# A front and a layer border that transpose the residual itself, in a two-layer f32 trunk on one core

## The chip, the core and the metric

The kernel runs on one core of a Trainium2 chip. Five engines work side by side: TensorE (PE in the profile; its weight loads are PEld), VectorE (DVE), ScalarE (ACT), GpSimd (POOL) and SyncE (SP), which only issues transfers. Matmuls write PSUM, of which the kernel uses eight banks of 128 x 512 f32; everything else stands in SBUF. The metric is device microseconds of the whole program; lower is better.

## The reference, cut to what matters

```
h = rms_norm(x, norm_pre[layer])                 # x: (1, 512, 2048) f32
even layer: z = h @ w_in (2048 x 7168): qa, fa, ia, ga, ub, vb, gb
            8 recurrence heads from qa, fa, ia (values), gate ga
            8 spatial-gating groups from ub, vb (layer-normed), gate gb
            y = concat @ w_out (2048 x 2048)
odd layer:  z = h @ w_in: cq (512), ckv (512), kpe (64), gate (2048)
            q = rms_norm(cq) @ w_qb,  kv = rms_norm(ckv) @ w_kvb
            16 heads of causal attention, times silu(gate);  y = o @ w_out
x = x + rms_norm(y, norm_post[layer])
```

`rms_norm(x, w)` multiplies each row by one factor r = (mean(x^2) + eps)^-0.5 and each column by w. Both factors can be put elsewhere: w into the rows of the next weight matrix, r onto the rows of the product.

## The kernel before

All large products are made with three matmuls on operands split in two parts of type fp32r: high x high, high x low, low x high. The activations' transposes stand in `R`, 32 slots of 128 x 512, high and low part for each of 16 blocks k of the model dimension. Weights come in tiles of 128 x 1024 f32 (`raw`, three buffers, 512 KB each), are cast to `whi` on ACT (L168) and their remainder `wlo` is made on DVE (L169), four buffers each; `piece(n)` asks for tile n + 3 before tile n is used.

Products of two kinds are made. `proj_tok` (L209 to L211) holds four row blocks of 128 tokens as weights of the array and streams 256 or 512 columns of the weight matrix: the values ia, vb, cq, ckv and both output projections. `proj_feat` (L214 to L216) holds the weight matrix and streams 512 tokens: fa, qa, ga, ub, gb and the gate. A 512 wide `proj_tok` takes four `mm` banks, all there are with that name; `sc` and `tp` have two each.

The front: for each of four row blocks `pre_norm` squares four chunks of x (L290), adds (L292), forms the factor on POOL (L275, L276), multiplies by factor and norm weight on DVE (L296), transposes 16 times on PE (L301) and splits into `R` (L283, L284). The norm weight is loaded into four partitions and spread by stream shuffles. Head values are projected in three chunks: pair 0 with 256 columns, pairs 1 and 2 together with 512, pair 3 with 256. The first chunk runs with its first four weight tiles in one group, row block by row block.

The border: `out_proj` makes the even layer's output in four chunks of 512 columns. Each evacuation squares (L674) and multiplies by the post-norm weight (L675). After the last chunk of a row block, `last_evac` adds the squares (L680), forms the factor on POOL, adds the residual (L684), stores x1 and calls `pre_norm` for the odd layer, whose scaling and transposes are put off by six to seven ticks (`DEFER`); a tick passes with each weight tile or part of a group. The chunk cq follows.

Nobody writes the order out: the framework's scheduler places instructions on each engine by priority and by its own estimate of when they can run; the `at(delay, ...)` tasks only set where they are handed to it. All DMAs go through SP in one queue.

## Time and profile before

| | us |
|---|---|
| median of 3 runs (lowest, highest) | 1597.62 (1597.39, 1598.52) |
| profiled execution: its own time | 1596.93 |
| its span, first to last instruction | 1595.2 |
| PE busy | 1568.3 |
| DVE busy | 750.8 |
| ACT busy | 532.0 |
| POOL busy | 95.7 |

A row of the groups reads: line, engine, operation, output<-inputs, shape, count | busy us, mean ns of one | idle time of the engine just before them and what ended it. A row of the timeline begins with the start and the duration in us. Matmul ends are modelled, so the step from start to start tells more than a duration. Numbers Lnnn are lines of the kernel before; the order of the changed kernel has its own line numbers.

### The profile page before, as it was taken

To read this page: it belongs to the slowest core of one execution; us is meant where nothing else is said; L and a number is where in the kernel's file an instruction comes from. 1 tells how busy PE (TensorE), PEld (TensorE's weight loads), DVE (VectorE), ACT (ScalarE), POOL (GpSimd) and SP (SyncE) were. 2 spreads that over 40 slices of the span, in tenths; PEclk is the share of its full clock that TensorE was granted. 3 is DMA by queue.
4 is the path that set the end of the run, shared out by engine and by line. 5 is a ranking of instruction groups with operands and counts; after the bars stand their busy time and mean duration, and the time that the engine had idled before them with its cause. 6 is when DMAs were issued, how large, how long until landed. Compare 5 with 4: busy or idle time off the path is not lost. (4 is left out here: it accounts for less than half of the span.)

```text
span 1595.2 us, 19593 instructions
## 1 busy us (share of the span) xinstructions
PE 1568.3 (98%) x7841; PEld 1327.2 (83%) x7841; DVE 750.8 (47%) x1333; ACT 532.0 (33%) x904; POOL 95.7 (6%) x145
## 2 busy tenths in 40 slices
PE   6999999999999999999999999999999999999997
PEld 6888888898888888888887788888889988988886
DVE  7653455535434224353225743232266767762234
ACT  6422322222222222232224533222265555542221
POOL 1000000000014004000001000000000000000000
PEclk9999999999999999999999999999999999999999
DMA  7332222223234333243335523333221221332324
GB/s 221 118 92 80 92 93 80 80 80 99 91 102 119 99 98 101 94 151 100 102 103 172 150 78 102 93 93 98 87 75 55 70 60 52 102 106 94 105 93 158
DMA packets 118150, 160.95 MB, mean 101 GB/s; under 512 B 7830, under 2 KB 74408, under 8 KB 118056
## 3 DMA queue, kind: packets, MB, share of 16 engines
q1 hardware_dynamic: 118060, 159.71, 32.4%
q8 instruction: 61, 1.00, 0.3%
q14 instruction: 29, 0.24, 0.0%
HBM read 151.30 MB, written 8.39 MB: 100 GB/s over the span
## 5 line engine op out<-in xcount | busy, mean ns | idle before, releaser
L169 DVE TENSOR_TENSOR wlo<-raw,whi 128x1024 fp32r<-128x1024 f32 x240 | 296.8, 1238 | 641.3 <-ACT whi L168 624.8
L168 ACT CAST whi<-raw 128x1024 fp32r<-128x1024 f32 x240 | 252.3, 1052 | 779.1 <-PE mm L211 346.3
L209 PE MATMUL mm<-whi,R 128*128 128x512 f32 (+1 forms) x960 | 364.0, 379 | 0.5 <-ACT R L283 0.5
L210 PE MATMUL mm<-wlo,R 128*128 128x512 f32 (+1 forms) x960 | 362.1, 377 | 1.2 <-DVE wlo L169 1.2
L211 PE MATMUL mm<-whi,R 128*128 128x512 f32 (+1 forms) x960 | 362.1, 377 | 0.0
L214 PE MATMUL mm<-R,whi 128*128 128x512 f32 x832 | 326.1, 392 | 0.0
L216 PE MATMUL mm<-R,wlo 128*128 128x512 f32 x832 | 324.0, 389 | 0.0
L215 PE MATMUL mm<-R,whi 128*128 128x512 f32 x832 | 323.9, 389 | 0.0
L210 PEld LDWEIGHTS mm<-wlo,R 128*128 128x128 f32 x960 | 181.6, 189 | 33.3 <-DVE wlo L169 2.0
L209 PEld LDWEIGHTS mm<-whi,R 128*128 128x128 f32 x960 | 181.6, 189 | 33.0 <-ACT R L283 1.2
L211 PEld LDWEIGHTS mm<-whi,R 128*128 128x128 f32 x960 | 181.5, 189 | 32.5
L216 PEld LDWEIGHTS mm<-R,wlo 128*128 128x128 f32 x832 | 156.1, 188 | 32.6
L214 PEld LDWEIGHTS mm<-R,whi 128*128 128x128 f32 x832 | 156.2, 188 | 32.2
L215 PEld LDWEIGHTS mm<-R,whi 128*128 128x128 f32 x832 | 156.2, 188 | 32.0
L214 PE MATMUL mm<-Wc,whi 128*128 128x512 f32 x160 | 62.9, 393 | 0.0
L216 PE MATMUL mm<-Wc,wlo 128*128 128x512 f32 x160 | 62.6, 391 | 0.0
L215 PE MATMUL mm<-Wc,whi 128*128 128x512 f32 x160 | 62.4, 390 | 0.0
L284 DVE TENSOR_TENSOR R<-mm,R 128x512 fp32r<-128x512 f32 x48 | 32.9, 686 | 27.9 <-ACT R L283 27.9
L284 DVE TENSOR_TENSOR R<-tp,R 128x512 fp32r<-128x512 f32 x64 | 42.3, 684 | 4.2 <-ACT R L283 3.5
L283 ACT CAST R<-tp 128x512 fp32r<-128x512 f32 x64 | 35.9, 587 | 20.4 <-PE tp L301 18.2
L896 ACT ACTIVATE G<-sc,nm 128x512 f32<-128x512 f32 (+2 forms) x48 | 26.1, 545 | 41.2 <-DVE nm L895 41.2
L283 ACT CAST R<-mm 128x512 fp32r<-128x512 f32 x48 | 28.2, 587 | 32.2 <-PE mm L211 18.3
(243 smaller groups left out, 1645.9 us busy)
## 6 DMA issues: line engine op xcount, KB each, us to landing
raw<-in_ev_w_in_dram SPq DMA_DIRECT2D x112, 512.0 KB, 3.6
raw<-in_od_w_in_dram SPq DMA_DIRECT2D x49, 512.0 KB, 3.8
raw<-in_ev_w_out_dram SPq DMA_DIRECT2D x32, 512.0 KB, 3.6
raw<-in_od_w_out_dram SPq DMA_DIRECT2D x32, 512.0 KB, 3.7
raw<-in_od_w_kvb_dram SPq DMA_DIRECT2D x16, 512.0 KB, 3.6
raw<-in_od_w_qb_dram SPq DMA_DIRECT2D x16, 384.0 KB, 3.2
Wa<-in_x_dram SPq DMA_DIRECT2D x16, 256.0 KB, 6.3
G<-in_x_dram SPq DMA_DIRECT2D x16, 256.0 KB, 4.2
```

Source lines behind the costliest of these rows:

```text
L168: nc.scalar.copy(hi[:, 0:n], raw[:, 0:n])
L169: nc.vector.tensor_tensor(lo[:, 0:n], raw[:, 0:n], hi[:, 0:n].bitcast(F32), ALU.subtract)
L209: nc.tensor.matmul(o, hh[:, sl], wh, start=first, stop=False, skip_group_check=True)
L210: nc.tensor.matmul(o, hh[:, sl], wl, start=False, stop=False, skip_group_check=True)
L211: nc.tensor.matmul(o, hl[:, sl], wh, start=False, stop=last, skip_group_check=True)
L214: nc.tensor.matmul(ps, hi, hh, start=first, stop=False)
L215: nc.tensor.matmul(ps, hi, hl, start=False, stop=False)
L216: nc.tensor.matmul(ps, lo, hh, start=False, stop=last)
L283: nc.scalar.copy(dst_hi, src)
L284: nc.vector.tensor_tensor(dst_lo, src, dst_hi.bitcast(F32), ALU.subtract)
L896: nc.scalar.activation(pv[j], sp[j], AF.Exp, bias=nm[:, j:j + 1], scale=C_SCALE, accum_out=su[:, j:j + 1])
```

## The change

*Raw-block front.* x is transposed as it is. `flip_x` transposes two 128 x 128 blocks, ACT scales them by the norm weight while it casts them into `R` (a column per partition, `ncol`), DVE makes the low parts. `first_chunk` runs the first value chunk, now 512 wide, in eight pieces of four turns; a turn has six matmuls, one flip ahead and, in four of the pieces, a square. Six and eight idle transposes of the identity stand at its beginning. The row factor rn is known after the seventh piece; it is applied in each evacuation of the even layer, as an ACT scale, or as a DVE multiplication by `rb`, the factor spread over all partitions by four small matmuls. The layer norm of vb takes eps times the mean square instead. Values are projected 512 wide for pairs 0 and 1, and 2 and 3.

*Border.* The last output chunk's second half and the first half of cq run in eight turns written by hand, one row block each; the transposes (`flip_x1`) read the sum x1 itself. The odd layer's norm weight is multiplied into its weight tiles (`normed`), the row factor goes into the evacuations and, for cq and ckv, into the epsilon of their norms.

*Order.* Inside the two stretches `in_order` ties every PE, ACT and DVE instruction to the one traced before it; several loads are held in program order on SP. Setup of masks, rope and columns is handed over later.

```diff
+    def in_order():
...
+        for ins in traced[start:]:
+            if ins.engine in (mybir.EngineType.PE, mybir.EngineType.Activation, mybir.EngineType.DVE):
+                if ins.engine in prev:
+                    tc.add_manual_dep(ins, prev[ins.engine],
+                                      mybir.DependencyInfo(mybir.DependencyClass.NoSync,
+                                                           mybir.DependencyReason.DATA), reason="in_order")
+                prev[ins.engine] = ins.name
...
-    for c in range(4):
-        (nc.vector if c % 2 else nc.gpsimd).memset(B[:, 4 + c, :], 0.0)
-    nc.sync.dma_start(out=B[0:P:32, 4:8, :],
-                      in_=norm_pre[0].partition_broadcast(4).rearrange("q (c n) -> q c n", c=4))
-    for c in range(4):
-        nc.sync.dma_start(out=W[:, c, :], in_=x_t[0][:, c * 512:(c + 1) * 512])
+    nrow = B[0:16, 0, 0:P]
+    nc.sync.dma_start(out=nrow, in_=norm_pre[0].rearrange("(k p) -> k p", p=P))
+    def load_x(i, c):
+        tc.keep_in_program_order(nc.sync.dma_start(out=W[:, 4 * i + c, :],
+                                                   in_=x_t[i][:, c * 512:(c + 1) * 512]))
+    load_x(0, 0)
...
+        if i in norm_k:
+            for kk in range(nk):
+                e = slice(kk * nco, (kk + 1) * nco)
+                w = cols[:, 18 + norm_k[i] + kk:19 + norm_k[i] + kk]
+                nc.scalar.activation(hi[:, e], raw[:, e], AF.Copy, scale=w)
+                nc.vector.scalar_tensor_tensor(lo[:, e], raw[:, e], w, hi[:, e].bitcast(F32),
+                                               ALU.mult, ALU.subtract)
...
+        if cuts is None or cuts == "halves":
...
+    def square(i, c):
+        nc.scalar.activation(G[:, 7, :], W[:, 4 * i + c, :], AF.Square, scale=D ** -0.5,
+                             accum_out=pss[:, i, c:c + 1])
+    def factor():
+        nc.vector.tensor_reduce(rms[:, 2], pss, AX.X, ALU.add)
+        nc.gpsimd.tensor_scalar(rms[:, 2], rms[:, 2], EPS, None, ALU.add)
+        nc.gpsimd.tensor_tensor(rn, rms[:, 2], mhalf[:, 0:4], ALU.pow)
+        nc.gpsimd.tensor_scalar(eps_rn, rms[:, 2], EPS, None, ALU.mult)
+    def spread_rn():
+        tp = tp_bank()
+        for i in range(NT):
+            nc.tensor.matmul(tp[:, i * P:(i + 1) * P], rn[:, i:i + 1].broadcast_to([P, P]), ident,
+                             start=True, stop=True)
+        nc.scalar.copy(rb, tp)
+    def flip_x(n):
+        q, i = n // NT, n % NT
+        if q > 7:
+            return
+        tp = tp_bank()
+        sl = slice(i * P, (i + 1) * P)
+        for j in range(2):
+            o = (2 * q + j) % 4 * P
+            nc.tensor.transpose(tp[:, j * P:(j + 1) * P], W[:, 4 * i + q // 2, o:o + P], ident)
+        parts = [(2 * q + j, ncol[:, 2 * q + j:2 * q + j + 1], tp[:, j * P:(j + 1) * P]) for j in range(2)]
+        for k, w, src in parts:
+            nc.scalar.activation(R[:, 2 * k, sl], src, AF.Copy, scale=w)
+        for k, w, src in parts:
+            nc.vector.scalar_tensor_tensor(R[:, 2 * k + 1, sl], src, w, R[:, 2 * k, sl].bitcast(F32),
+                                           ALU.mult, ALU.subtract)
+    def first_chunk(first, evac):
+        outs = [mm_bank() for _ in range(NT)]
+        ntp = sc_bank()
+        nc.tensor.transpose(ntp[:, 0:KD], nrow, ident[0:KD, 0:KD])
+        nc.vector.tensor_copy(ncol, ntp[:, 0:KD])
+        def idle_turns(n):
+            for _ in range(n):
+                nc.tensor.transpose(ntp[:, P:2 * P], ident, ident)
+        idle_turns(6)
+        flip_x(0)
+        idle_turns(8)
+        issue_to(first)
+        flips = iter(range(1, 8 * NT + 4))
+        for q in range(8):
+            if q + 3 < 8:
+                fetch(first + q + 3)
+            if q < 2:
+                for t in range(NT):
+                    load_x(t, 2 + q)
+            for i in range(NT):
+                if q > 0 or i > 1:
+                    flip_x(next(flips))
+                mms(q, i, 0)
+                if q == 0 and i < 2:
+                    flip_x(next(flips))
+                mms(q, i, 1)
+                if q == 0 and i < 2:
+                    flip_x(next(flips))
+                if i == (0 if q else 1) and q < 7:
+                    issue_to(first + q + 1)
+                if q in (1, 3, 4, 6):
+                    square(i, {1: 0, 3: 1, 4: 2, 6: 3}[q])
+                if q == 7:
+                    evac(i, outs[i])
+            if q == 6:
+                factor()
+            tick()
...
-        if p == 1:
-            pl["ia", p] = plan_chunk(ew, IA + 256, 512, KD, 2)
-        elif p != 2:
-            pl["ia", p] = plan_chunk(ew, IA + 256 * p, 256, KD, 4)
+        if p % 2 == 0:
+            pl["ia", p] = plan_chunk(ew, IA + 256 * p, 512, KD, 2, "halves" if p == 0 else None)
...
-    wpre = [B[:, 4 + c, :] for c in range(4)]
-    for c in range(4):
-        nc.vector.stream_shuffle(wpre[c], wpre[c], [0] * 32)
+    fetch(0)
+    for i in range(1, NT):
+        load_x(i, 0)
+    fetch(1)
     for i in range(NT):
-        if i > 0:
-            for c in range(4):
-                nc.sync.dma_start(out=W[:, 4 * i + c, :], in_=x_t[i][:, c * 512:(c + 1) * 512])
-            if i == 1:
-                issue_to(3)
-        else:
-            for q in range(2):
-                fetch(q)
-        pre_norm(i, [W[:, 4 * i + c, :] for c in range(4)], wpre,
...
+        load_x(i, 1)
+        if i == 1:
+            fetch(2)
...
+                nc.scalar.activation(G[:, vp:vp + 2, i * P:(i + 1) * P], psv[:, a:a + 2], AF.Copy,
+                                     scale=rn[:, i:i + 1])
         def fa_evac(m, ps):
+            nc.vector.tensor_tensor(ps, ps, rb, ALU.mult)
             nc.scalar.activation(W[:, m, :], ps, AF.Sigmoid)
             nc.scalar.activation(W[:, 2 + m, :], ps, AF.Sigmoid, scale=-1.0)
         def qa_evac(m, ps):
-            nc.scalar.copy(W[:, 4 + m, :], ps)
+            nc.vector.tensor_tensor(W[:, 4 + m, :], ps, rb, ALU.mult)
...
         if p == 0:
-            at(1, setup_cols)
-            at(12, setup_rope)
-        if p != 2:
-            proj_tok(pl["ia", p], 512 if p == 1 else 256, r_act, KD, ia_evac, by="first" if p == 0 else "piece")
+            at(2, setup_masks)
+            at(7, load_pk)
+            at(9, spread_rn)
+            at(11, setup_cols)
+            at(16, setup_rope)
+            with in_order():
+                first_chunk(pl["ia", p], ia_evac)
+        elif p == 2:
+            proj_tok(pl["ia", p], 512, r_act, KD, ia_evac)
...
-                nc.scalar.copy(U[:, m], ps)
+                nc.vector.tensor_tensor(U[:, m], ps, rb, ALU.mult)
             def gb_evac(m, ps, p=p, Z=Z, V=V):
+                nc.vector.tensor_tensor(ps, ps, rb, ALU.mult)
...
+        def last_sum(i, ps):
             evac(i, ps, 1536, 3)
...
+            rs[i] = rstd_of(s1, D, 1, "yrs")
+        def last_add(i):
...
+                nc.vector.scalar_tensor_tensor(ch[c], ch[c], rs[i], resid[i][c], ALU.mult, ALU.add)
+            finish(i, ch)
             if i + 2 < NT:
                 load_resid(i + 2)
...
+    def flip_x1(i, c):
+        tp = tp_bank() if c % 2 else sc_bank()
+        for j in range(4):
+            nc.tensor.transpose(tp[:, j * P:(j + 1) * P], W[:, 4 * i + c, j * P:(j + 1) * P], ident)
+        sl = slice(i * P, (i + 1) * P)
+        split_into(R[:, 8 * c:8 * c + 8:2, sl], R[:, 8 * c + 1:8 * c + 8:2, sl],
+                   tp.rearrange("p (j t) -> p j t", j=4))
+    def square_x1(i, c):
+        nc.scalar.activation(G[:, 8, :], W[:, 4 * i + c, :], AF.Square, scale=D ** -0.5,
+                             accum_out=pss[:, i, c:c + 1])
...
+    def border(eo, last_sum, last_add):
+        cq = pl["cq"]
+        turns = {(1, 2): [(flip_x1, 0, 0)], (1, 3): [(flip_x1, 0, 1)],
+                 (2, 2): [(flip_x1, 1, 0)], (2, 3): [(flip_x1, 1, 1)],
+                 (4, 1): [(flip_x1, 0, 2)], (4, 2): [(flip_x1, 0, 3)],
+                 (5, 0): [(flip_x1, 2, 0)], (5, 1): [(flip_x1, 2, 1), (last_add, 3)],
+                 (5, 2): [(flip_x1, 1, 2)], (5, 3): [(flip_x1, 1, 3)],
+                 (6, 0): [(flip_x1, 3, 0)], (6, 1): [(flip_x1, 3, 1)],
+                 (6, 2): [(flip_x1, 2, 2)], (6, 3): [(flip_x1, 2, 3)],
+                 (7, 0): [(flip_x1, 3, 2), (issue_to, cq + 4)], (7, 1): [(flip_x1, 3, 3), (issue_to, cq + 5)],
+                 (7, 2): [(issue_to, cq + 6)],
+                 (1, 0): [(last_add, 0)], (2, 0): [(last_add, 1)], (4, 0): [(last_add, 2)]}
+        for j in range(4):
+            turns[3, j] = [(issue_to, cq + j), (fetch, cq + 3 + j)]
...
+        issue_to(eo + 7)
+        for n in range(3):
+            fetch(cq + n)
+        with in_order():
+            for turn in range(8):
+                for j in range(4):
+                    if turn < 4:
+                        mms(outs, eo, 4 + j, turn)
+                    else:
+                        mms(cq_outs, cq, j, turn - 4)
+                    for fn, *args in turns.get((turn, j), ()):
+                        fn(*args)
+                    if j == 3 and turn < NT:
+                        last_sum(turn, outs[turn])
+                    if turn >= NT:
+                        square_x1(turn - NT, j)
+                    tick()
+            factor_x1()
...
+        if first:
+            for q in range(4, 8):
+                wh, wl = piece(pl[name] + q)
...
+                tick()
+        else:
+            proj_tok(pl[name], 512, r_act, KD, evac)
+        r = sm.tile([P, 4], F32, name="lrs")
+        nc.gpsimd.tensor_tensor(r, ss, eps_rn1, ALU.add)
+        nc.gpsimd.tensor_tensor(r, r, mhalf[:, 0:4], ALU.pow)
...
+    spread_rn1()
...
+            nc.vector.tensor_tensor(ps, ps, rb, ALU.mult)```

PE at the start, before (tp: transposed x; mm: the chunk's bank; whi, wlo: parts of the weight tile):

```order
L301 MATMUL tp_123<-ident_90,B_77 128x128 x4
L301 MATMUL tp_131<-ident_90,B_77 128x128 x4
L209 MATMUL mm_332<-whi_158,R_76 128x256
L210 MATMUL mm_332<-wlo_159,R_76 128x256
L301 MATMUL tp_139<-ident_90,B_77 128x128 x4
L211 MATMUL mm_332<-whi_158,R_76 128x256
```

and in the change (sc: a bank for the norm column and the idle transposes; Wa: x as loaded):

```order
L407 MATMUL sc_120<-ident_83,B_77 128x16
L412 MATMUL sc_120<-ident_83 128x128 x6
L390 MATMUL tp_129<-ident_83,Wa_80 128x128 x2
L412 MATMUL sc_120<-ident_83 128x128 x8
L251 MATMUL mm_116<-whi_144,R_76 128x512
L252 MATMUL mm_116<-wlo_145,R_76 128x512
L253 MATMUL mm_116<-whi_144,R_76 128x512
L390 MATMUL tp_159<-ident_83,Wa_80 128x128 x2
```

The transposes read loaded x (Wa) and no longer the scaled copy (B), and come two at a time between threes of matmuls.

ACT at the start, with what each instruction waits for, before:

```order
L290 ACT_TABLE_LOAD
L290 ACTIVATE G_78,pss_112<-Wa_80 128x512 [waits DMAHW0_49]
L290 ACTIVATE G_78,pss_112<-Wa_80 128x512 [waits DMAHW1_49,Activation_49]
L290 ACTIVATE G_78,pss_112<-Wa_80 128x512 [waits DMAHW3_49,Activation_49]
L290 ACTIVATE G_78,pss_112<-Wa_80 128x512 [waits DMAHW4_49,Activation_49]
L168 CAST whi_158<-raw_108 128x1024 [waits DMAHW0_49]
```

and in the change (DVE_49: DVE's counter, here the copy into ncol):

```order
L393 ACT_TABLE_LOAD [waits DVE_49]
L393 ACTIVATE R_76<-tp_129,ncol_90 128x128 [waits PE_49]
L393 ACTIVATE R_76<-tp_129,ncol_90 128x128
L210 CAST whi_144<-raw_97 128x512 [waits DMAHW2_49]
L210 CAST whi_144<-raw_97 128x512
L393 ACTIVATE R_76<-tp_159,ncol_90 128x128 [waits PE_49]
```

The table load had no wait and now stands behind one; the weight cast follows the first flip.

DVE at the border, from the last output chunk's first row block on, before (yrs, prs: row factors; B in L296: the scaled copy):

```order
L675 TENSOR_TENSOR Wa_80<-mm_5706,B_77 128x512
L680 TENSOR_REDUCE ys1_5880<-yss_4905 128x1
L684 SCALAR_TENSOR_TENSOR Wa_80<-Wa_80,yrs_5882,G_78 128x512 x4
L292 TENSOR_REDUCE ps1_5902<-pss_5897 128x1
L296 SCALAR_TENSOR_TENSOR B_77<-Wa_80,prs_5904,B_77 128x512
L675 TENSOR_TENSOR Wa_80<-mm_5707,B_77 128x512
```

and in the change (sc, tp: the transposed sum):

```order
L806 TENSOR_TENSOR Wa_80<-mm_5649,B_77 128x512
L813 TENSOR_REDUCE ys1_5811<-yss_4848 128x1
L819 SCALAR_TENSOR_TENSOR Wa_80<-Wa_80,yrs_5813,G_78 128x512 x4
L326 TENSOR_TENSOR R_76<-sc_5846,R_76 128x4x128
L326 TENSOR_TENSOR R_76<-tp_5859,R_76 128x4x128
L806 TENSOR_TENSOR Wa_80<-mm_5650,B_77 128x512
```

Between the residual sum and the split of its transposes no norm sum and no scaling stands any more.

More of the change, by code (lines that the diff above doesn't have):

```diff
@@ L1 @@
-from contextlib import ExitStack
+from contextlib import ExitStack, contextmanager
 import numpy as np
@@ L117, in setup_cols @@
         tp = tp_bank()
-        nc.tensor.transpose(tp[:, 0:18], pk, ident[0:18, 0:18])
-        nc.scalar.copy(cols, tp[:, 0:18])
+        nc.tensor.transpose(tp[:, 0:34], pk, ident[0:34, 0:34])
+        nc.scalar.copy(cols, tp[:, 0:34])
         e = sm.tile([P, 4, 8], F32, name="lbt", bufs=1)
@@ L166, in wload @@
         lo = ring.tile([P, 1024], F32R, name="wlo", tag="wlo")
-        if cuts is None:
-            nc.scalar.copy(hi[:, 0:n], raw[:, 0:n])
-            nc.vector.tensor_tensor(lo[:, 0:n], raw[:, 0:n], hi[:, 0:n].bitcast(F32), ALU.subtract)
+        if i in norm_k:
[5 more added lines that the diff above has]
+                                               ALU.mult, ALU.subtract)
+            return (hi[:, 0:n].rearrange("p (k c) -> p k c", k=nk),
+                    lo[:, 0:n].rearrange("p (k c) -> p k c", k=nk))
+        if cuts is None or cuts == "halves":
+            step = n if cuts is None else n // 2
+            for a in range(0, n, step):
+                e = slice(a, a + step)
+                nc.scalar.copy(hi[:, e], raw[:, e])
+                nc.vector.tensor_tensor(lo[:, e], raw[:, e], hi[:, e].bitcast(F32), ALU.subtract)
         else:
@@ L702, in out_proj @@
             proj_tok(pl[name, c], 512, r_act, KD, lambda i, ps, c=c: evac(i, ps, c * 512, c))
-        proj_tok(pl[name, 3], 512, r_act, KD, last_evac, by="last")
+        if border:
+            border(pl[name, 3], last_sum, last_add)
+        else:
+            proj_tok(pl[name, 3], 512, r_act, KD, last_evac, by="last")
+    rn1, eps_rn1 = rms[:, 0], rms[:, 1]
     def finish0(i, ch):
-        if i == 0:
-            for c in range(4):
-                row_bc(B[:, 4 + c, :], norm_pre[1, c * 512:(c + 1) * 512])
@@ new lines, in square_x1, with factor_x1, spread_rn1 @@
+    def square_x1(i, c):
+        nc.scalar.activation(G[:, 8, :], W[:, 4 * i + c, :], AF.Square, scale=D ** -0.5,
+                             accum_out=pss[:, i, c:c + 1])
+    def factor_x1():
+        nc.vector.tensor_reduce(rms[:, 2], pss, AX.X, ALU.add)
+        nc.gpsimd.tensor_scalar(rms[:, 2], rms[:, 2], EPS, None, ALU.add)
+        nc.gpsimd.tensor_scalar(eps_rn1, rms[:, 2], EPS, None, ALU.mult)
+        nc.gpsimd.tensor_tensor(rn1, rms[:, 2], mhalf[:, 0:4], ALU.pow)
+    def spread_rn1():
+        tp = tp_bank()
+        for i in range(NT):
+            nc.tensor.matmul(tp[:, i * P:(i + 1) * P], rn1[:, i:i + 1].broadcast_to([P, P]), ident,
+                             start=True, stop=True)
+        nc.scalar.copy(rb, tp)
```

118 lines of the change are left out of this document (83 added, 35 removed).

## The prediction

> **What bounds the kernel now.** I read the page first, then the order of time at the start, then the groups of instructions around the border of the two layers.
>
> ```profile
> span 1595.2 us, 19593 instructions
> PE 1568.3 (98%) x7841; PEld 1327.2 (83%) x7841; DVE 750.8 (47%) x1333; ACT 532.0 (33%) x904; POOL 95.7 (6%) x145
> PE   6999999999999999999999999999999999999997
> GB/s 221 118 92 80 92 93 80 80 80 99 91 102 119 99 98 101 94 151 100 102 103 172 150 78 102 93 93 98 87 75 55 70 60 52 102 106 94 105 93 158
> ```
>
> TensorE (PE) is the bound in all slices but the first and the last. DVE, the next engine, has less than half the load. So only three things can move the time: PE's own work, the stretches where it waits, and the stretch in which it runs slowly. What DVE and ACT gain or lose counts only where PE waits for it. The digit 9 hides small losses, so I price work by the spacing of starts:
>
> ```profile
> 0.79 0.87 SPq L100 DMA_DIRECT2D Wa<-in_x_dram  x2
> 3.95 0.63 ACT L290 ACTIVATE G<-Wa 128x512 f32<-128x512 f32 x1 [1.88 <-DMA Wa<-in_x_dram]
> 10.69 1.97 PE L301 MATMUL tp<-ident,B 128*128 128x128 f32 x8 [10.69 <-DVE B L296]
> 12.48 0.58 PE L209 MATMUL mm<-whi,R 128*128 128x256 f32 x1
> 15.18 0.56 PE L211 MATMUL mm<-whi,R 128*128 128x256 f32 x1
> 17.25 0.41 PE L210 MATMUL mm<-wlo,R 128*128 128x256 f32 x1
> 17.46 0.41 PE L211 MATMUL mm<-whi,R 128*128 128x256 f32 x1
> 19.80 0.28 PE L210 MATMUL mm<-wlo,R 128*128 128x256 f32 x1
> 30.38 0.60 PE L301 MATMUL tp<-ident,B 128*128 128x128 f32 x4
> 46.76 0.28 PE L209 MATMUL mm<-whi,R 128*128 128x256 f32 x1
> 48.92 0.40 PE L214 MATMUL mm<-R,whi 128*128 128x512 f32 x1
> 899.77 0.40 PE L209 MATMUL mm<-whi,R 128*128 128x512 f32 x1
> 902.98 0.39 PE L211 MATMUL mm<-whi,R 128*128 128x512 f32 x1
> L541 PE MATMUL tp<-ident,G 128*128 128x128 f32 x32 | 4.8, 272 | 0.0
> ```
>
> Prices: from 899.77 to 902.98 lie 14 steps of a 512 wide matmul, so 0.229 us each. From 46.76 to 48.92 lie 18 steps of a 256 wide one, 0.120 each: more than half. Four transposes take 0.60 with a last one of 0.272, so a step is (0.60-0.272)/3 = 0.109. Until about 19.8 the same 256 wide matmul steps by 0.21 (17.25 to 17.46): PE runs slowly at first.
>
> **The front's loss.** The 256 wide first chunk has 192 matmuls (16 k, 4 row blocks, 3 products) and 64 transposes: 192 x 0.120 + 64 x 0.109 = 30.0 us. Its successor L214 starts at 48.92. So 18.9 us are lost: 10.69 before PE's first instruction, the rest in slow clock and waits.
>
> **The border's loss**, over 40 us around the seam (busy, mean ns, idle before):
>
> ```profile
> L209 PE MATMUL mm<-whi,R 128*128 128x512 f32 x40 | 16.3, 407 | 0.5 <-ACT R L283 0.5
> L211 PE MATMUL mm<-whi,R 128*128 128x512 f32 x39 | 15.8, 405 | 0.0
> L210 PE MATMUL mm<-wlo,R 128*128 128x512 f32 x39 | 15.5, 398 | 0.0
> L301 PE MATMUL tp<-ident,B 128*128 128x128 f32 x60 | 9.5, 280 | 3.6 <-DVE B L296 3.2 <-DVE R L284 0.3
> ```
>
> 118 x 0.229 + 60 x 0.109 = 33.6 of 40: 6.4 us lost, mostly where transposes wait for the DVE multiplication L296, which needs the whole row's norm.
>
> **The change part by part.** *Work of PE.* Head values were projected in chunks of 256, 512, 256 columns and now in two of 512: 384 x 0.120 - 192 x 0.229 = 2.1 us less. Two spreads of the row factor add 8 small f32 matmuls at about 0.11 each: 0.9 more. Transposes of x and of the border stay 64 each. Net -1.2.
>
> *Front, start.* The prices I use, all in one place (DVE and ACT rows, then landings):
>
> ```profile
> L517 DVE SCALAR_TENSOR_TENSOR G<-G,btot,sc 128x128 f32<-128x128 f32 x16 | 5.4, 338 | 0.7 <-ACT G L515 0.6
> L296 DVE SCALAR_TENSOR_TENSOR B<-Wa,prs,B 128x512 f32<-128x512 f32 x32 | 23.1, 745 | 3.7 <-POOL prs L276 3.7
> L178 DVE TENSOR_TENSOR wlo<-raw,whi 128x512 fp32r<-128x512 f32 x16 | 11.0, 687 | 18.9 <-ACT whi L177 18.9
> L430 DVE COPY G<-Wa 128x32 f32<-128x32 f32 x8 | 1.5, 194 | 0.1
> L515 ACT COPY G<-sc 128x128 f32<-128x128 f32 x8 | 2.1, 258 | 0.0
> L896 ACT ACTIVATE G<-sc,nm 128x128 f32<-128x128 f32 x16 | 5.9, 367 | 9.9 <-DVE nm L895 9.9
> L896 ACT ACTIVATE G<-sc,nm 128x512 f32<-128x512 f32 x16 | 11.0, 689 | 28.7 <-DVE nm L895 28.7
> L177 ACT CAST whi<-raw 128x512 fp32r<-128x512 f32 x16 | 10.0, 623 | 20.7 <-PE mm L215 19.8 <-ACT G L896 0.9
> L290 ACT ACTIVATE G<-Wa 128x512 f32<-128x512 f32 x32 | 20.2, 632 | 10.0 <-DVE Wa L684 6.7 <-DMA Wa<-in_x_dram 2.7
> L290 ACT ACTIVATION_READ_ACCUMULATOR G<-Wa 128x1 f32 x32 | 6.0, 187 | 0.0
> L290 ACT ACT_TABLE_LOAD x1 | 1.3, 1283 | 0.8 <-PEq L984 0.8
> raw<-in_od_w_in_dram SPq DMA_DIRECT2D x49, 512.0 KB, 3.8
> Wa<-in_x_dram SPq DMA_DIRECT2D x16, 256.0 KB, 6.3
> pk<-in_ev_lb_logits_dram SPq DMA_DIRECT2D x1, 8.0 KB, 3.4
> ```
>
> SP issues the norm row first, then one x chunk, then the weights, 0.43 us apart (0.87 for two). Before, the first load was issued at 0.79 and used at 3.95, so 3.1 us; the small row lands by 3.9. A transpose and a copy (0.19) make ncol at 4.4. ACT's table load now stands behind that copy and no longer at 0.78: it ends at 5.7. PE meanwhile does six slow idle transposes (0.21 each) and the first flip, to 6.1. ACT scales two 128 wide pieces (0.31 each, between 258 and 367) to 6.8 and casts half the weights to 7.4; PE's eight further idle transposes end at 7.8; the lower half of the split is there at 8.2, one slow matmul later. So first real matmul at 7.8 instead of 12.48. Bounds: nothing excludes that the small row lands a microsecond sooner than a whole x chunk, which gives 6.9; weights that take 6.3 like the median of x, from 1.7, land at 8.0, are cast by 8.6 and give 8.7.
>
> *Front, slow clock.* Before, PE stepped slowly until 19.8: 9.1 us after its first instruction, 4.6 after 15.18, where real matmuls follow each other without a stop. I take the latter: slow until 7.8 + 4.6 = 12.4, half of 4.6 lost, 2.3. Bounds: 0.5 if the idle transposes from 4.2 count as such work, 4.6 if 9.1 us are needed after 7.8.
>
> [...]
>
> *Front, waits.* Each of 32 turns has six matmuls and two transposes: 6 x 0.229 + 2 x 0.109 = 1.59. ACT has 2 x 0.31 for the flip and a quarter of two half casts (0.31): 0.93. In 16 turns comes a square of 0.82 (632 + 187): 1.75, that is 0.16 too long. Flips run two to three turns ahead, and the next four turns give it back, so 0 to 2.6 us; I take 1.5. DVE has 2 x 0.34 + 2 x 0.69/4 = 1.02 per turn and fits. Loads: x and the first eight weight tiles are 8.4 MB over 50 us, 168 GB/s, and the first 40 us ran at 221 before (the row GB/s); a turn's x chunk is asked for at least two loads ahead.
>
> Front: 7.8 + 2.3 + 1.5 = 11.6 less 0.2 for the flip counted twice, against 18.9: -7.5. L214's successor should start at 11.4 + 44.0 + 7.0 = 62.4.
>
> *Border.* Transposes now read the residual sum itself, so the square, the sum and the power of the next norm leave the path. What stays:
>
> ```profile
> 854.60 0.15 DVE L680 TENSOR_REDUCE ys<-yss 128x1 f32<-128x4 f32 x1
> 854.83 0.19 POOL L275 TENSOR_SCALAR yrs<-ys 128x1 f32<-128x1 f32 x1 [224.35 <-DVE ys L680]
> 855.11 0.56 POOL L276 TENSOR_TENSOR yrs<-yrs,mhalf 128x1 f32<-128x1 f32 x1
> 855.69 2.74 DVE L684 SCALAR_TENSOR_TENSOR Wa<-Wa,yrs,G 128x512 f32<-128x512 f32 x4 [0.95 <-POOL yrs L276]
> ```
>
> Square 0.8, product 0.69 and these rows give the first 512 columns about 3.3 us after a turn's end; their transposes stand 18 matmuls, 4.1 us, behind it. On SP's queue the sixteen stores and reloads of the first two row blocks (16 x 0.43 = 6.9 us, each behind its sum) stand ahead of the fourth q piece; they end about 1.8 us into turn 3. That piece is the tightest load: its buffer is free 3.6 us into turn 3 (1.4 for PE, 0.7, 1.5), it lands 3.8 + 0.4 later at 7.8, ACT has half of it at 8.5; PE wants it at 5.5 + 18 x 0.229 + 0.9 = 10.5. While ACT and DVE stand in that wait, the last row block's square and the third row's sum queue behind them; with 2 us in hand PE sees nothing. The stall that L296 made goes nowhere else: next in line would be the transposes of row block 2, in turn 5, which need the sum made in turn 4, with a whole turn between. I leave 0.5 of 6.4: -5.9. Bounds: 0, and 2 if the piece lands after 6.3 like x.
>
> *Costed at nothing.* 56 evacuations get a DVE product with rb (0.687 each, 38.5 us), and of the 48 weight tiles that now carry the norm's scale 16 are split in two pieces and 32 in four, 112 more DVE instructions at a fixed cost of about 0.2 (338 at 128 wide, 745 at 512), 22 us; the 32 products L296 (23.1) go. A fifth table load falls to ACT at the first gate evacuation. The cover is DVE's idle half; if it is gone, 38.5 us are at stake.
>
> **Sum.** -1.2 - 7.5 - 5.9 = -14.6. Span 1595.2 to 1580.6; the profiled execution 1596.93 to 1582.3; that execution lies 0.7 under the median 1597.62, so **1583.0**.
>
> **Rivals.** (a) The idle transposes open the clock: slow cost 0.5, not 2.3: 1581.2. For it: they fill PE from 4.2 on. Against: before, transposes from 10.69 did not hasten it visibly. (b) The front is paced by ACT: if a narrow scaled copy costs half a microsecond, 16 turns need 2.13 and lose 8.6 instead of 1.5: 1590.1; at the full 689 of the wide row it would be 16.3: 1597.8. Against: the 258 and 367 rows. (c) The front's start does not move (ncol, then the table load, later than I think): first matmul at 12.5, 1587.7. (d) Slower: rb's products hold PSUM banks, and PE waits at the opening of each second projection; fully exposed 38.5 us, 1621.5. It decides once an evacuation ends more than one projection (96 x 0.229 = 22 us) late; DVE's 47% speaks against it.
>
> **Chances.** Forecast 0.58, with its own range 1578 to 1587; (a) 0.20; (b) 0.12; (c) 0.06; (d) 0.04. The range 1577 to 1591 leaves out (d), the upper third of (b) and tails of the forecast. Within 0.2% (3.2 us, what a measurement of this kernel can tell from no change): only the top of (b), 0.03; slower: (d) and something unforeseen, 0.05; faster 0.92.
>
> **What would show it.** First 512 wide matmul near 7.8 and a step of 0.229 from about 12.4; the first feature-major matmul near 62.4; no PE wait over 0.5 us between the last output chunk and the kpe projection; DVE busy up by some 25 to 45 us with no new PE wait behind it. Wrong if flips wait for ACT turn after turn, or if PE waits for a bank after a gate.

## The result and the profile after

| | us |
|---|---|
| before, median of the runs beside it (lowest, highest) | 1597.51 (1596.74, 1598.52) |
| after, median of 4 runs (lowest, highest) | 1581.58 (1580.85, 1583.46) |
| ratio | 0.9902, 95% interval 0.9887 to 0.9916 |
| profiled execution of the change, span | 1580.85, 1579.1 |

In one later experiment a single run that took twice the time of all others is left out.

The change is faster by 15.9 us, within 1.5 us of the forecast. The page of the changed kernel, its sums and PE's slices:

```profile
span 1579.1 us, 19573 instructions
PE 1565.7 (99%) x7680; PEld 1318.0 (83%) x7680; DVE 788.2 (50%) x1512; ACT 559.8 (35%) x1059; POOL 95.5 (6%) x133
PE   9999999999999999999999999999999999999997
```

The 6 in the first slice has become a 9. DVE carries 37.4 us more than before and PE does not show it.

The front, from the timeline of the changed kernel, PE first:

```profile
2.46 0.26 PE L407 MATMUL sc<-ident,B 16*128 16x16 f32 x1 [2.46 <-DMA B<-in_norm_pre_dram]
2.99 1.54 PE L412 MATMUL sc<-ident 128*128 128x128 f32 x6 [0.27 <-DVE ncol L408]
5.28 0.69 PE L390 MATMUL tp<-ident,Wa 128*128 128x128 f32 x2 [0.75 <-DMA Wa<-in_x_dram]
5.76 1.91 PE L412 MATMUL sc<-ident 128*128 128x128 f32 x8
7.52 0.79 PE L251 MATMUL mm<-whi,R 128*128 128x512 f32 x1
8.25 0.50 PE L252 MATMUL mm<-wlo,R 128*128 128x512 f32 x1
8.58 0.39 PE L253 MATMUL mm<-whi,R 128*128 128x512 f32 x1
12.39 0.44 PE L390 MATMUL tp<-ident,Wa 128*128 128x128 f32 x2 [0.43 <-DVE R L395]
59.97 0.39 PE L256 MATMUL mm<-R,whi 128*128 128x512 f32 x1
```

and ACT in the same microseconds:

```profile
3.02 1.28 ACT L393 ACT_TABLE_LOAD   x1 [3.02 <-DVE ncol L408]
6.00 0.63 ACT L393 ACTIVATE R<-tp,ncol 128x128 fp32r<-128x128 f32 x2 [1.70 <-PE tp L390]
6.85 1.14 ACT L210 CAST whi<-raw 128x512 fp32r<-128x512 f32 x2 [0.22 <-DMA raw<-in_ev_w_in_dram]
```

The norm row has landed at 2.46, x at 5.28, the weights at 6.85; the first real matmul starts at 7.52, and from 8.25 on PE steps at full pace (0.23 from 8.58 to 8.81). The successor of the first chunk starts at 59.97. With 192 x 0.229 + 64 x 0.109 = 51.0 us of work ahead of it, the front loses 9.0 us where it lost 18.9: 9.9 gained.

The border, 842 to 882 us, groups of PE by line, in the changed kernel:

```profile
L251 PE MATMUL mm<-whi,R 128*128 128x512 f32 x50 | 20.8, 416 | 0.0
L252 PE MATMUL mm<-wlo,R 128*128 128x512 f32 x49 | 19.2, 392 | 0.0
L253 PE MATMUL mm<-whi,R 128*128 128x512 f32 x49 | 19.2, 392 | 0.0
L858 PE MATMUL tp<-ident,Wa 128*128 128x128 f32 x28 | 4.2, 272 | 0.0
L858 PE MATMUL sc<-ident,Wa 128*128 128x128 f32 x28 | 4.2, 272 | 0.0
```

148 x 0.229 + 56 x 0.109 = 40.0 of 40 us: by this sum nothing is lost, where 6.4 were. By the spacing of starts one small stall is left (0.27 us at 865.6; see the run with doubled rb products). The transposes wait for nobody.

### The profile page after: what moved, and what is told of

Same layout as the page of the kernel before. It is cut to its first block, busy times and chain, and to the rows that moved or that the text cites. A ratio compares the mean times of both kernels' runs of the same rounds, so it can differ in the third digit from the quotient of the medians.

```text
span 1579.1 us, 19573 instructions
## 1 busy us (share of the span) xinstructions
PE 1565.7 (99%) x7680; PEld 1318.0 (83%) x7680; DVE 788.2 (50%) x1512; ACT 559.8 (35%) x1059; POOL 95.5 (6%) x133
## 2 busy tenths in 40 slices
PE   9999999999999999999999999999999999999997
## 4 chain that ended last, share of the span: by engine, by line
PE 98%; DVE 1%; DMA 0%; ACT 0%; issue 0%; DVEq 0%; POOLq 0%; SPq 0%; POOL 0%; ACTq 0%
PE mm L256 14%; PE mm L258 14%; PE mm L257 14%; PE mm L253 14%; PE mm L251 14%; PE mm L252 14%; PE tp L1148 1%; PE sc L258 1%; PE sc L256 1%; PE sc L257 1%; PE sc L612 1%; PE tp L1159 1%; PE tp L1160 1%; PE tp L1161 1%; PE sc L618 1%; PE tp L390 0%
## 5 line engine op out<-in xcount | busy, mean ns | idle before, releaser
L211 DVE TENSOR_TENSOR wlo<-raw,whi 128x1024 fp32r<-128x1024 f32 (+1 forms) x200 | 238.9, 1198 | 458.8 <-ACT whi L210 443.0
L210 ACT CAST whi<-raw 128x1024 fp32r<-128x1024 f32 (+1 forms) x200 | 202.8, 1018 | 623.6 <-PE mm L253 286.5
L251 PE MATMUL mm<-whi,R 128*128 128x512 f32 x896 | 354.9, 396 | 0.0
L253 PE MATMUL mm<-whi,R 128*128 128x512 f32 x896 | 349.4, 390 | 0.0
L252 PE MATMUL mm<-wlo,R 128*128 128x512 f32 x896 | 349.3, 390 | 0.0
L256 PE MATMUL mm<-R,whi 128*128 128x512 f32 x832 | 326.5, 392 | 0.0
L258 PE MATMUL mm<-R,wlo 128*128 128x512 f32 x832 | 324.1, 390 | 0.0
L253 PEld LDWEIGHTS mm<-whi,R 128*128 128x128 f32 x896 | 168.2, 188 | 35.3 <-DVE R L395 0.2
L252 PEld LDWEIGHTS mm<-wlo,R 128*128 128x128 f32 x896 | 168.5, 188 | 33.8 <-DVE wlo L211 0.4
L251 PEld LDWEIGHTS mm<-whi,R 128*128 128x128 f32 x896 | 168.4, 188 | 33.1 <-ACT whi L210 0.2
L258 PEld LDWEIGHTS mm<-R,wlo 128*128 128x128 f32 x832 | 156.2, 188 | 32.7
L256 PEld LDWEIGHTS mm<-R,whi 128*128 128x128 f32 x832 | 156.2, 188 | 32.0
L202 DVE SCALAR_TENSOR_TENSOR wlo<-raw,cols,whi 128x256 fp32r<-128x256 f32 (+1 forms) x160 | 77.0, 535 | 103.2 <-ACT whi L201 103.2
L201 ACT ACTIVATE whi<-raw,cols 128x256 fp32r<-128x256 f32 (+1 forms) x160 | 77.1, 542 | 116.1 <-issue 64.3
L256 PE MATMUL mm<-Wc,whi 128*128 128x512 f32 x160 | 62.9, 393 | 0.0
L258 PE MATMUL mm<-Wc,wlo 128*128 128x512 f32 x160 | 62.6, 391 | 0.0
L326 DVE TENSOR_TENSOR R<-mm,R 128x512 fp32r<-128x512 f32 x48 | 33.0, 687 | 27.7 <-ACT R L325 27.7
L325 ACT CAST R<-mm 128x512 fp32r<-128x512 f32 x48 | 28.2, 587 | 31.9 <-PE mm L253 18.3
```

The lines of the kernel that those rows point to most:

```text
L201: nc.scalar.activation(hi[:, e], raw[:, e], AF.Copy, scale=w)
L202: nc.vector.scalar_tensor_tensor(lo[:, e], raw[:, e], w, hi[:, e].bitcast(F32), ALU.mult, ALU.subtract)
L210: nc.scalar.copy(hi[:, e], raw[:, e])
L211: nc.vector.tensor_tensor(lo[:, e], raw[:, e], hi[:, e].bitcast(F32), ALU.subtract)
L251: nc.tensor.matmul(o, hh[:, sl], wh, start=first, stop=False, skip_group_check=True)
L252: nc.tensor.matmul(o, hh[:, sl], wl, start=False, stop=False, skip_group_check=True)
```

## The experiments

The kernels ran beside the kernel before in three groups (its medians 1597.03, 1597.30 and 1597.39). "The clock opens" means the moment from which PE is granted its full clock (in the kernel with 30 transposes the granted clock was 0.50 from 12 to 20 us, and a 256 wide matmul stepped by 0.21, after the opening at 21.60 by 0.12); the moments named below are read from the trace's record of the granted clock. The "successor" is the first matmul behind the first value chunk. Where times of two changed kernels are compared, the spread of one kernel, 0.7 to 2.6 us, is the bound on what can be told.

### The front alone

The new front, with the border, the weight tiles and the evacuations of layer 1 as before:

```
-    pl["cq"] = plan_chunk(ow, CQ, 512, KD, 2, normed=True)
+    pl["cq"] = plan_chunk(ow, CQ, 512, KD, 2)
...
-    out_proj(W, "eo", norm_post[0], x_t, G[:, 8, :], finish0, border=border)
+    out_proj(W, "eo", norm_post[0], x_t, G[:, 8, :], finish0)
```

> The new front and the two 512 wide value chunks, with the border of before (the row factor applied in pre_norm, order left to the scheduler). Theory, by places: the front lost 18.9 us before and loses 9.0 in the change, the value chunks save 2.1, the spread of the row factor takes back 0.9, so about 10.6 of the 16 us: 1587; the border still loses 6 us between the last output chunk and cq. Rival, that the border's gain comes with the front (less DVE work, shifted loads): 1583 or below.

Measured: 1587.63 (1586.10 to 1587.89), 0.9938 of the kernel before [0.9921, 0.9955]: 9.4 us less. Its border, 842 to 882 us (40 of the 64 transposes lie in it):

```profile
L250 PE MATMUL mm<-whi,R 128*128 128x512 f32 x44 | 17.7, 403 | 0.5 <-ACT R L324 0.5
L342 PE MATMUL tp<-ident,B 128*128 128x128 f32 x40 | 6.4, 282 | 3.4 <-DVE B L337 3.2 <-DVE R L325 0.2
```

The waits for the scaled copy are all back. The front gives its gain without the border's help.

### The border alone

The old front, with the eight turns, the scaled weight tiles and rb's products of the change:

```
-        proj_tok(pl[name, 3], 512, r_act, KD, last_evac, by="last")
+        if border:
+            border(pl[name, 3], last_sum, last_add)
+        else:
+            proj_tok(pl[name, 3], 512, r_act, KD, last_evac, by="last")
```

> The new border (transposes of the sum itself, eight turns, norm weight in the weight tiles, row factor in the evacuations) behind the front of before. Theory: 6.4 us of lost time go, 0.9 for the spread matmuls comes: 1592, and the front still loses 18.9. Rival, that the two parts need each other: within 2 us of before.

Measured: 1592.04 (1591.23 to 1592.11), 0.9967 [0.9954, 0.9980]: 5.0 us less. In its profile PE has no stall at the border; the old front ended 0.8 us later than in the profile of before (successor at 49.70 instead of 48.92), and its first matmul came at 13.94 and not at 12.48. So the two parts give 9.4 and 5.0, 14.4 together, and 15.9 were measured with both. The parts add up to within the spread of one kernel.

### No idle transposes

```
-        idle_turns(6)
         flip_x(0)
-        idle_turns(8)
```

> The change without its 14 idle transposes. In the changed kernel the granted clock is full from 8.3 us, 0.7 after the first real matmul. Theory 1: the idle transposes opened it; without them PE's dense work begins at 7.5 and the clock opens 4.6 to 6 us later, at 12 to 13.5, and half of that is lost: 1584. Theory 2, that transposes do not count and the clock opened by itself: it opens before 9 again and the time stays at 1581.6.

Measured: 1583.02 (1582.14 to 1583.59), 0.9911 [0.9897, 0.9926]. PE in the timeline of this kernel:

```profile
5.34 0.69 PE L390 MATMUL tp<-ident,Wa 128*128 128x128 f32 x2 [2.52 <-DMA Wa<-in_x_dram]
7.59 0.80 PE L251 MATMUL mm<-whi,R 128*128 128x512 f32 x1 [1.56 <-ACT whi L210]
11.90 0.63 PE L252 MATMUL mm<-wlo,R 128*128 128x512 f32 x1
12.33 0.63 PE L253 MATMUL mm<-whi,R 128*128 128x512 f32 x1
14.03 0.39 PE L253 MATMUL mm<-whi,R 128*128 128x512 f32 x1
```

The first matmul starts as early as in the change (7.59), but the step from 11.90 to 12.33 is 0.43 where 0.229 is full pace, and full pace begins only at 14.0. So the idle transposes do not bring the first matmul forward; they bring the clock forward, from 14.0 to 8.3 in these two profiles (in other profiles of the same front it opens as late as 11.67, as shown below). The successor starts at 62.35, 2.4 later. The medians differ by 1.4, but the runs of the two kernels overlap, so the trace carries this and not the time alone.

### No held order at the border, and none at the front

In the first kernel the border, in the second the front, is written as in the change but not tied:

```
-        with in_order():
+        if True:
```

> The change with the border's eight turns traced the same way but not tied in order, so that the scheduler places the instructions. Theory: what the border gained comes from transposing the sum itself, so that no norm stands in the way; the order by hand is worth 2 us at most: 1581.6 to 1583.6. Rival: the tied order is what gains, and the scheduler brings back 4 to 6 us of waits for transposes: 1585.6 to 1588.

Measured: 1583.29 (1583.10 to 1584.27), 0.9915 [0.9900, 0.9930]. In its profiled execution (1584.27) the clock opened at 11.67, which costs (11.67 - 8.26) x 0.5 = 1.7 us at the front, and PE stalled 1.5 us at the border for a late weight tile, against 0.3 in the change. The first part has nothing to do with the order. For the second, the transfers on SP, first of the free border, then of the change:

```profile
861.84 3.02 SPq L177 DMA_DIRECT2D raw<-in_od_w_in_dram  x3
859.02 8.09 SPq L177 DMA_DIRECT2D raw<-in_od_w_in_dram  x4
```

Counted from the border's first transpose (848.23 here, 846.59 in the change) the late tile is asked for at 13.6 and not at 12.4. Its buffer is freed by weight splits on DVE, and in the free order a residual sum (L819) stands ahead of them: they begin at 12.2 and not at 11.0. The tile then takes 5.7 us to land. Two kernels with the held order in which it took 5.6 and 5.9 us (nine idle transposes with smaller loads, and no idle transposes) lost 0.5 and 0.6 there, so the order is worth about 1 us in this profile. It is one profile, and the time alone does not show it.

> The 32 turns of the front are written as before, but their order is no longer held: the instructions of PE, ACT and DVE are placed by what they depend on. On ACT the squares of a row block then stand ahead of the cast of a weight tile and of flips, and on PE a flip's transposes are parted. Theory (the held order is what keeps the flips two turns ahead of their matmuls): an ACT square costs 0.82 us by the rows of the kernel before and now stands in front of a flip that PE wants; some eight of the 32 flips come late by half of that, so 1584 to 1588, with waits of PE for R inside the first 60 us. Rival (the order hardly matters, since ACT and DVE have slack in the front): within 1 us of 1581.6, and no wait of PE over 0.5 us between 10 and 60 us.

Measured: 1585.96 (1585.32 to 1586.96), 0.9930 [0.9913, 0.9946]. The time falls where it was expected, the place does not. The timeline of this kernel, of DVE, PE and ACT:

```profile
7.63 1.29 DVE L211 TENSOR_TENSOR wlo<-raw,whi 128x512 fp32r<-128x512 f32 x2 [5.85 <-ACT whi L210]
8.84 0.17 DVE L408 COPY ncol<-sc 128x16 f32<-128x16 f32 x1
9.06 1.54 PE L412 MATMUL sc<-ident 128*128 128x128 f32 x6 [3.10 <-DVE ncol L408]
12.42 0.61 ACT L393 ACTIVATE R<-tp,ncol 128x128 fp32r<-128x128 f32 x2
12.82 0.80 PE L251 MATMUL mm<-whi,R 128*128 128x512 f32 x1 [0.29 <-ACT R L393]
```

The copy that makes ncol, 0.17 us long and ready to go at 2.7, stands behind the weight split on DVE, which waits 5.85 us for a transfer and a cast. So ncol comes at 9.0 and the first matmul at 12.82 instead of 7.52. In between PE makes its 14 idle transposes, which write the bank that the copy reads, at half clock; ACT, with a square and a weight cast ahead of the first scaled copy, holds PE up for another 0.29. After that no wait of PE over 0.5 us follows; the later flips are on time although squares stand ahead of them. The held order is worth 4.4 us, nearly all of it at the start and through one small instruction in one queue, and not through the later flips that I had in mind.

### Twice the rb products

```
+            nc.vector.tensor_scalar(ps, ps, 1.0, None, ALU.mult)
             nc.vector.tensor_tensor(ps, ps, rb, ALU.mult)
```

ahead of each of the 56 evacuations that carry rb.

> Each of the 56 evacuations of layer 1 that carry the product with the row factor rb gets one more DVE multiplication of the same bank (by 1.0) ahead of it, about 0.5 us each, 27 us of DVE in all. Theory (DVE's idle half covers rb's products, as the prediction costed them at nothing): 1581.6, within 1.5, DVE busy about 815 and no new wait of PE for a bank. Rival (the products hold PSUM banks, prediction's case (d)): part of the 27 us shows, up to 1608.

Measured: 1582.58 (1581.79 to 1583.12), 0.9906 [0.9889, 0.9922]. Forty of the evacuations lie in layer 0, between 82 and 688 us, and not in layer 1 as I wrote; the other sixteen are the gate's, from 988 us on. One kind of evacuation in the groups of this kernel, the added product first:

```profile
L1029 DVE TENSOR_SCALAR mm<-mm 128x512 f32<-128x512 f32 x16 | 11.2, 699 | 5.3 <-PE mm L258 5.3
L1030 DVE TENSOR_TENSOR mm<-mm,rb 128x512 f32<-128x512 f32 x16 | 11.1, 696 | 0.3
```

They cost 0.70 us each, not the 0.5 I had taken; DVE is busy 822.4, up 34. The median lies 1.0 above the change's, and the profiled execution (1583.12) 2.3 above the profiled one of the change (1580.85). The profile shows these 2.3 us in two places that the edit does not touch: the clock opened at 10.87 instead of 8.26 (1.3 us), and PE stalled at the border for 1.0 us more than in the change, 180 us after the last of layer 0's products and 120 before the gate's first:

```profile
867.82 0.50 PE L251 MATMUL mm<-whi,R 128*128 128x512 f32 x1 [0.59 <-ACT whi L201]
868.60 0.50 PE L252 MATMUL mm<-wlo,R 128*128 128x512 f32 x1 [0.28 <-DVE wlo L202]
```

PE has no new stall behind any of the 56. DVE's idle half covers the products, and twice as many.

That stall is the load which the prediction called the tightest, the fourth q piece. ACT's cast of it waits for the transfer, first in the change, then here:

```profile
864.54 1.34 ACT L201 ACTIVATE whi<-raw,cols 128x512 fp32r<-128x512 f32 x2 [3.66 <-DMA raw<-in_od_w_in_dram]
867.04 1.33 ACT L201 ACTIVATE whi<-raw,cols 128x512 fp32r<-128x512 f32 x2 [4.80 <-DMA raw<-in_od_w_in_dram]
```

In every kernel with the held border the load is asked for 12.4 to 12.5 us after the border's first transpose. Where the trace shows its landing, it took 4.6 to 6.6 us, and so the cast begins between 17.2 and 19.1; PE stalls where that is 17.9 or later and does not up to 17.5. By the spacing of starts PE lost 0.3 us there in the change, 0.2 in its repeat, nothing with nine idle transposes, and 1.3 here. I had taken 4.2 us for the landing and given the load 2 us in hand; it has none in some executions.

### Idle transposes in the kernel before

```
+    idle = sc_bank()
+    for _ in range(30):
+        nc.tensor.transpose(idle[:, 0:P], ident, ident)
```

> The kernel before, with 30 transposes of the identity on a spare bank ahead of its front, nothing else. [...] Rival (transposes do not count, and the spread of the opening between the runs with idle transposes was chance): opening at 17 to 20 and 1597.

Measured: 1598.43 (1597.24 to 1599.13), 1.0006 [0.9997, 1.0016]: no gain, where I had expected 2 to 4.5 us (0.09 us, from the steps of 0.21 and 0.12, on each of some 35 matmuls), and yet not as the rival says. PE in the timeline of this kernel, then its clock by stretches (the columns are the stretch, its length, busy time and count of PE, PEld, DVE, ACT, POOL, the granted clock, DMA share, GB/s):

```profile
2.49 6.14 PE L352 MATMUL sc<-ident 128*128 128x128 f32 x30 [2.49 <-POOL ident masks.py:199]
10.84 1.78 PE L301 MATMUL tp<-ident,B 128*128 128x128 f32 x8 [2.21 <-DVE B L296]
15.32 0.58 PE L209 MATMUL mm<-whi,R 128*128 128x256 f32 x1 [2.71 <-ACT R L283]
21.66 0.28 PE L211 MATMUL mm<-whi,R 128*128 128x256 f32 x1
```

```profile
10.00:12.00 2.00, 1.15 (x7) 0.92 (x8) 1.97 (x3) 0.31 (x1) 0.00 (x0) 0.84 0.92 265
12.00:14.00 2.00, 0.61 (x3) 0.21 (x1) 1.99 (x3) 1.60 (x2) 0.00 (x0) 0.50 1.05 394
20.00:22.00 2.00, 2.00 (x12) 2.00 (x12) 1.29 (x2) 2.00 (x5) 0.38 (x2) 0.60 0.98 268
```

The clock opened at 7.95, while PE had done nothing but transposes of the identity. Then PE idled 2.21 us, and the clock closed at 11.36 (0.84 of the stretch from 10 to 12: 1.36 us at full, 0.64 at half). It opened again at 21.60. From one turn of the clock to the next lie 3.41 and 10.24 us, one and three times 3.41. So in this profile transposes alone opened the clock, and it closed again 0.52 us after a gap of 2.21. In this kernel ACT's cast of the first transposes also stood behind two weight casts and a square, so the first matmul came at 15.32 instead of 12.48; the edit changed more than the clock.

### What opens the clock, read from all profiles

The stretch at full clock lasts 1563.30, 1566.72 or 1570.13 us in all profiles (that of the first opening with 30 transposes apart, 3.41): these too differ by 3.41. So I take 3.41 us as the measure, and list for each profile the idle time of PE in the 3.41 us that end at the opening, and in the 3.41 us before them (ends of matmuls are modelled, so a wait directly behind one is partly hidden):

| kernel | opens at | idle in the 3.41 us before it | in the 3.41 us before those |
|---|---|---|---|
| before | 19.77 | 0.00 | 0.77 |
| border alone | 19.40 | 0.00 | 0.68 |
| before + 30 transposes, first | 7.95 | 0.00 | 1.37 |
| before + 30 transposes, second | 21.60 | 0.00 | 0.55 |
| no idle transposes | 14.00 | 0.00 | 0.42 |
| free front | 13.89 | 0.29 | 2.00 |
| free border | 11.67 | 0.00 | 0.72 |
| twice rb | 10.87 | 0.00 | 0.88 |
| front alone | 10.66 | 0.00 | 0.97 |
| changed kernel | 8.26 | 0.44 | 1.62 |
| changed kernel, again | 10.74 | 0.00 | 0.78 |
| nine idle transposes | 8.31 | 0.20 | 1.30 |
| smaller first loads and nine | 6.39 | 0.07 | 3.16 |
| smaller first loads | 5.84 | 0.39 | 3.41 |

Ahead of every opening stand 3.41 us with at most 0.44 us of idle PE, and the 3.41 us before those have between 0.42 and 3.41. 0.42 stands on one side and 0.44 on the other, so the two are not parted sharply. Nor do 3.41 us without a gap suffice wherever they begin: without idle transposes PE ran without a gap from 7.59 on, and the clock opened at 14.00. What sets the moment is not shown. The opening differs from run to run: the front alone, the free border, twice rb and the change share one front, and open at 10.66, 11.67, 10.87 and 8.26. (The last four rows are of kernels that follow below.) That spread of 3.41 us is worth 1.7 us of time at half clock.

### Nine idle transposes, smaller first loads, both, and the change again

The change leaves a gap of 0.75 us between its six idle transposes and the first flip (4.53 to 5.28), and PE's start waits for transfers. Both can be edited:

```
-        idle_turns(6)
+        idle_turns(9)
...
-    load_x(0, 0)
+    tc.keep_in_program_order(nc.sync.dma_start(out=W[:, 0, 0:256], in_=x_t[0][:, 0:256]))
...
+        if n == 0:
+            for kk in range(nk):
+                tc.keep_in_program_order(nc.sync.dma_start(out=raw[:, kk * nco:(kk + 1) * nco], in_=src[:, kk]))
...
+        if i == 2:
+            tc.keep_in_program_order(nc.sync.dma_start(out=W[:, 0, 256:512], in_=x_t[0][:, 256:512]))
```

The first x chunk and the first weight tile come in halves; the second half of x follows the loads of two more x chunks.

First both together:

> The changed kernel with smaller first loads: the first x chunk as 256 columns ahead of the weights (its other half after the next x chunk), the first weight tile as two transfers of 256 KB, and nine instead of six idle transposes ahead of the first flip. Theory (PE's first matmul waits for transfers, x at 5.28 and the weight tile at 6.85, and a smaller one lands sooner): x at about 4.4 to 4.8, the first weight tile at about 5.8, first matmul at 6.6 to 7.0 instead of 7.5, so 0.5 to 0.9 us less: 1580.7 to 1581.1. Rival (a transfer's time is nearly its fixed part, or the queue's other transfers share the bandwidth): the first matmul stays at 7.4 to 7.8 and the time at 1581.6.

then each alone, and the changed kernel once more beside them:

> The changed kernel with nine idle transposes instead of six ahead of the first flip, nothing else. [...] Mean gain 1.7 us of clock, so 0.8 us of time: about 1580.7 against the changed kernel's 1581.6. Rival (the opening in the run with smaller loads came from the smaller loads, or by chance): opening again between 8.3 and 11.7, and 1581.6.

> The changed kernel with the smaller first loads alone (six idle transposes as in the changed kernel). [...] Rival (the smaller loads have the whole gain of the run that had both): 1580.3. Rival (they have none): 1581.6.

> The changed kernel once more, beside the two others on one chip. [...] Rival (the opening has a fixed time behind PE's first work): opening at 8.3 as in its first profile.

| kernel | median (lowest, highest) | ratio to before | first matmul | clock opens | successor |
|---|---|---|---|---|---|
| change, again | 1581.94 (1581.23, 1582.60) | 0.9902 [0.9888, 0.9917] | 7.65 | 10.74 | 61.21 |
| nine idle | 1581.18 (1580.26, 1581.72) | 0.9897 [0.9880, 0.9913] | 7.63 | 8.31 | 60.13 |
| smaller loads | 1579.96 (1579.68, 1580.34) | 0.9890 [0.9876, 0.9905] | 6.28 | 5.84 | 59.02 |
| both | 1580.34 (1580.02, 1581.17) | 0.9893 [0.9878, 0.9908] | 6.88 | 6.39 | 59.37 |

The change again, PE in its timeline:

```profile
7.65 0.80 PE L251 MATMUL mm<-whi,R 128*128 128x512 f32 x1
8.97 0.63 PE L253 MATMUL mm<-whi,R 128*128 128x512 f32 x1
10.95 0.38 PE L390 MATMUL tp<-ident,Wa 128*128 128x128 f32 x2
```

The same program as at the top, and its clock opens at 10.74 instead of 8.26: the rival of a fixed time behind PE's first work falls. The 3.41 us ahead of this opening have no idle PE, and those before them (3.91 to 7.33) 0.78 us, the whole gap; in the first profile 0.44 of the gap's 0.75 us lie in the 3.41 ahead of the opening. The successor is later by 1.24, half of the 2.48.

Nine transposes leave 0.20 us of the gap, and the opening, 8.31, lies at the lower edge of the rival's span. No run shows the mean gain of 1.7 us of clock that I had counted on: the change opened at 8.26 in one profile and at 10.74 in the other. The time is 0.8 less than the change's, as expected, but the runs of the two overlap, so neither the time nor the opening settles it.

Smaller loads alone, PE in the timeline of that kernel:

```profile
3.08 1.54 PE L416 MATMUL sc<-ident 128*128 128x128 f32 x6 [0.27 <-DVE ncol L412]
4.42 0.63 PE L394 MATMUL tp<-ident,Wa 128*128 128x128 f32 x2
4.85 1.53 PE L416 MATMUL sc<-ident 128*128 128x128 f32 x8
6.28 0.50 PE L255 MATMUL mm<-whi,R 128*128 128x512 f32 x1
```

x has landed before the sixth idle transpose ends: the flip follows without a gap at 4.42, and the first matmul comes at 6.28, 1.4 us sooner than in the change beside it. The clock opened at 5.84, ahead of the first real matmul. This is the fastest kernel of all: its slowest run (1580.34) lies below the fastest of the change beside it (1581.23), 2.0 us in the medians, though the intervals of the ratios to before still overlap. I had expected 1581.0 for it; the rival that it has the whole gain held. How the 2.0 us divide between the sooner start and the sooner clock is not shown: against the first profile of the change, whose clock opened at 8.26, the successor comes 0.95 sooner, against the repeat 2.19. With nine transposes on top, three of them only hold up a flip whose data is there (first matmul 6.88, as expected; the time, 1580.34, is below the 1580.7 to 1581.1 expected).

## Why the prediction was right, point by point

**Work of PE**: -1.2 forecast, about -0.35 by the rows of the trace. The wider chunks stand at their 2.1 by the forecast's prices; no run has them alone. The spreads cost twice what I took:

```profile
L378 PE MATMUL tp<-ident,rms 128*128 128x128 f32 x8 | 1.1, 274 | 0.0
L876 PE MATMUL tp<-ident,rms 128*128 128x128 f32 x8 | 1.1, 274 | 0.0
```

Each spread has four matmuls in the program and eight in the trace: 16 steps of 0.109, 1.75 us, and not 0.9. This term was mis-sized.

**Front, start**: first matmul forecast 7.8, measured 7.52, but by another chain. I let ncol come at 4.4 and the table load end at 5.7, both on the path; the small row had landed at 2.46 and the table load was over at 4.30, hidden. What set the start was x at 5.28, flip and scaling to 6.6, then the weights at 6.85. I had both there in time. Two errors cancelled. The smaller loads bear it out: with x and the first weights sooner, the first matmul came sooner by 1.24 us (6.28).

**Front, slow clock**: this step failed. I forecast 2.3 us lost, slow until 12.4, since before the clock had opened 4.6 us after continuous matmuls began. Measured: slow until 8.26, 0.4 us lost, which is rival (a), and until 10.74 in the repeat, 1.5 lost. The reason that I gave against (a), that transposes from 10.69 had not hastened the opening before, did not hold: behind them and the first matmul (from 13.06) lay a gap of 0.75 us, every opening in the table above has at most 0.44 us of idle PE in the 3.41 ahead of it, and with 30 transposes the clock opened at 7.95 with nothing but transposes before it. That the gap cost the opening, and not the kind of instruction, is my reading of these numbers; no run has the kernel before without that gap. The 4.6 us were no constant: one front opened between 8.26 and 11.67, and that the first profile shows 8.26, so far below 12.4, is in part luck. Without idle transposes the opening came at 14.0, later than my 12.4.

**Front, waits**: 1.5 forecast. Measured 9.0 - 7.52 - 0.4 + 0.2 = 1.3, but not as squares that push flips late: part is the second matmul's delay for the first wlo (the step from 7.52 to 8.25 is 0.73, where a slow one is 0.43), 0.43 is a flip's wait for its bank at 12.39, and no turn after that waits over 0.5. The pair of scaled copies took 0.63, the 0.31 each that I took, so rival (b) had no ground. The successor came at 59.97 (forecast 62.4) and at 61.21 in the repeat.

**Border**: 0.5 left of 6.4 forecast, 0.3 measured, in the place named: the fourth q piece. The margin of 2 us which I gave that load was too generous: it landed after 4.6 to 6.6 us and not after 4.2, and stalled PE by 1.3 us in the run with doubled products; the bound of 2 for a late landing holds it.

**Costed at nothing**: DVE up by 37.4 us, which is 38.5 + 22 - 23.1 of the forecast. That it agrees to the tenth is luck: in busy time the weight splits came about 19 dearer, not 22, and the low parts of x, now in 64 pieces of 128 columns (19.4 us) where 16 of 512 stood (10.9), were left out. Rows of the changed kernel behind it:

```profile
L202 DVE SCALAR_TENSOR_TENSOR wlo<-raw,cols,whi 128x256 fp32r<-128x256 f32 x128 | 54.4, 482 | 80.8 <-ACT whi L201 80.8
L395 DVE SCALAR_TENSOR_TENSOR R<-tp,ncol,R 128x128 fp32r<-128x128 f32 x64 | 19.4, 344 | 20.1 <-ACT R L393 19.9
L1024 DVE TENSOR_TENSOR mm<-mm,rb 128x512 f32<-128x512 f32 x16 | 11.2, 700 | 10.6 <-PE mm L258 10.6
```

Rival (d) fell with the doubled products, rival (c) with the first matmul at 7.52.

**The sum**: -7.5 became -9.9, -5.9 became -6.1, -1.2 became -0.35: -16.3 against a span that fell by 16.1. Of the front's 2.4 us beyond the forecast 1.9 are the clock, 0.3 the start and 0.2 the waits; the spreads took 0.85 back. The median, 1581.58, lies nearer to the 1581.2 of rival (a) than to the forecast's 1583.0. In the repeat, with its later clock, the front gained 8.7, nearer the forecast of 7.5.
